# Low parts of weights in the mixers and the memory part: an accumulating DMA onto a negated high part in place of a subtraction

## The chip, the cores and the metric

The program runs on one core of a Trainium2 chip. A core has a matrix engine (TensorE, PE in the profile; its weight loads are the row PEld), a vector engine (VectorE, DVE), a scalar engine (ScalarE, ACT), a general engine (GpSimd, POOL) and a sync engine (SyncE, SP) that here issues the transfers. The metric is the time of one execution on the device in microseconds, less is better.

## The reference

Two encoder layers over x (512 tokens, 1024 features) with a memory of 256 tokens, then a final RMSNorm. All in float32.

```python
for i in range(DEPTH):                      # DEPTH = 2
    h = rms_norm(x, g_mix[i])
    if i % 2 == 0:                          # layer 0
        x = x + mixer_ab(h, w_in_ab[j], g_qa[j], g_ka[j], sink_b[j], w_out_ab[j], ang_1d, ang_2d)
    else:                                   # layer 1
        x = x + mixer_cd(h, w_in_cd[j], g_cq[j], g_ckv[j], w_uq[j], w_ukv[j], rpb_d[j], w_out_cd[j], ang_c)
    x = x + memory_cross_attention(rms_norm(x, g_xq[i]), rms_norm(mem, g_mem[i]),
                                   w_xq[i], w_xkv[i], w_xo[i])
    x = x + swiglu(rms_norm(x, g_ffn[i]), w_gate_up[i], w_down[i])
return rms_norm(x, g_final)
```

mixer_ab is two attentions side by side, A over all tokens with normed and rotated heads (8 heads, 2 of k and v) and B in a window of 128 tokens with a sink; both come from one input projection of 1536 columns and go through one output projection of 1024. mixer_cd is the same with C (latent attention, low-rank q and kv) and D (a 2-D neighbourhood with a bias). The cross-attention has 4 heads of 128 and projects the memory by w_kv (1024 x 1024) to keys and values. The FFN has 2816 columns for gate and as many for up.

## The kernel before

**Products of three.** Every float32 operand is split into a high part, which is the value rounded to the type float32r, and a low part, the rest. A product is three matmuls into one PSUM bank (`mm3`): high times high, high times low, low times high. On the profile's pages these are L127, L128 and L129.

**Weights.** `load` brings a piece of a weight matrix by one SP transfer into a tile `raw` (two buffers of 128 x 2048). `split` makes of 1024 columns of it the tiles `wh` and `wl`, each from a pool of four buffers: ACT copies raw to wh with the cast (L117), then DVE (one instruction) or POOL (four, one for each quarter) subtracts, wl = raw - wh (L123). So four splits can be in flight; a fifth waits until PE has read the buffer of the first for the last time. `alternate` takes turns between DVE and POOL where it is called: for the output projections ("op"), for the q and k weights of D ("dp") and for the memory's keys and values ("kv"). Everywhere else the low part is DVE's.

**Stages.** In each layer: norm of x and its split into xgh and xgl; input projection (by `natural_weights` and `natural` with tokens on the partitions, or, for D's q and k, by `proj_pair`); attention units that run score products, softmax (DVE, ACT, POOL), transposes of P on PE (L272) with a split of P into pth (ACT, L275) and ptl (DVE, L276), and PV products into the bank O (L550); `o_finish` (L236 ACT, L237 DVE) and the split of o into high (DVE, L293) and low (POOL, L294); output projection (`out_proj`), whose banks are added to x. The products on the memory (`memory_kv`, with casts of its results to kvh on ACT, L849) are run in the mixer, where PE has gaps. Then cross-attention and FFN, which have splits of their own for their weights. In layer 1 `v_d(0)` and `v_d(1)` are the values of D, their weights come from `natural_weights`.

**Order.** Each engine works through its instructions in a fixed order. It isn't that of the code: the framework simulates the program and sorts the instructions of all engines by the times that the simulation gives, so a change of one operation's kind can move others. PSUM has eight banks: two mm, two S, two T, one X and one O. SP issues only loads and stores and so runs ahead until a raw buffer is missing.

The line numbers here and in the rows are those of the kernel before; the changed kernel has them later in the file, by 11 behind `split` and by 15 behind `natural_weights`.

Of the kernel before, what the change touches and what calls it, by code (L numbers as in the profile page):

```python
# [11 lines left out]
F32R = mybir.dt.float32r  # L12
AF = mybir.ActivationFunctionType
ALU = mybir.AluOpType
# [3 lines left out]
P = 128  # L18
# [3 lines left out]
KF = D // P  # L22
# [9 lines left out]
def trunk_kernel(  # L32
# [6 lines left out]
    nc = tc.nc  # L39
# [4 lines left out]
    wp = ctx.enter_context(tc.tile_pool(name="wp", bufs=4))  # L44
    gp = ctx.enter_context(tc.tile_pool(name="gp", bufs=16))
    op = ctx.enter_context(tc.tile_pool(name="op", bufs=8))
# [51 lines left out]
    def load(src, a, b):  # L98
        raw = wp.tile([P, 2048], F32, tag="raw", bufs=2, name="raw")
        v = raw[:, :a * b].rearrange("p (a b) -> p a b", a=a)  # L100
        nc.sync.dma_start(v, src)
        return v
# [3 lines left out]
    def alternate(kind):  # L106

        turns[kind] = not turns.get(kind, False)
        return nc.vector if turns[kind] else nc.gpsimd

    def split(v, a, b, eng=None, low=nc.vector):
# [11 lines left out]
            low.tensor_sub(lv[:, q], v[:, q], hv[:, q].bitcast(F32))  # L123
        return hv, lv

    def mm3(o, lh, ll, rh, rl, start, stop):
        nc.tensor.matmul(o, lh, rh, start=start, stop=False)  # L127
        nc.tensor.matmul(o, lh, rl, start=False, stop=False)  # L128
        nc.tensor.matmul(o, ll, rh, start=False, stop=stop)  # L129
# [58 lines left out]
        return bc  # L188

    def natural_weights(w, c0, eng=None):  # L190
        v = load(w[:, c0:c0 + 256].rearrange("(k p) n -> p k n", p=P), KF, 256)
        return [split(v[:, 4 * i:4 * i + 4], 4, 256, eng) for i in range(2)]

    def natural(xh, xl, w, c0, evac, parts=None, bank_fn=None):

# [13 lines left out]
    def out_proj(os_, w, r0, after=None):  # L209

        nk = len(os_)
        for mg in range(2):
            v = load(w[r0:r0 + nk * P, mg * 512:(mg + 1) * 512]
                     .rearrange("(k p) n -> p k n", p=P), nk, 512)
            for mq in range(2):
                wh, wl = split(v[:, :, mq * 256:(mq + 1) * 256], nk, 256, None, alternate("op"))
                for m2 in range(2):
                    m = mg * 4 + mq * 2 + m2
                    bank = mm_bank()
                    cs = slice(m2 * P, (m2 + 1) * P)  # L220
                    for k in range(nk):
                        mm3(bank, wh[:, k, cs], wl[:, k, cs], *os_[k],
                            k == 0, k == nk - 1)
                    nc.vector.tensor_add(xs[m], xs[m], bank)
                    if after:
                        after(m)
# [78 lines left out]
    with tc.tile_pool(name="init", bufs=1) as ip:  # L305
# [17 lines left out]
        for f in range(KF):  # L323
            k = f % 2
            if f % 4 == 0:
                whl = [wp.tile([P, 1024], F32R, tag=t, name=t).rearrange("p (a b) -> p a b", a=4) for t in ("wh", "wl")]
            if k == 0:
                wh, wl = (t[:, f % 4:f % 4 + 2] for t in whl)
                v = raw[:, f:f + 2]
# [225 lines left out]
    def mixer_cd(normed, after):  # L555
# [3 lines left out]
        with tc.tile_pool(name="cd", bufs=2) as ph:  # L559
# [181 lines left out]
            def proj_pair(pr):  # L741

                if pr == 0:
                    qk = cT(4)
                else:
                    t = ph.tile([P, 4, S], F32R, tag="qk", bufs=2, name="dqk")
                    qk = [t[:, i] for i in range(4)]
                for w, c0, sc in ((0, 416, 0.125), (1, 928, 1.0)):
                    v = load(w_in[:, c0 + pr * P:c0 + (pr + 1) * P].rearrange("(k p) n -> p k n", p=P), KF, P)
                    wh, wl = split(v, KF, P, None, alternate("dp"))  # L750
                    bank = mm_bank()
                    for k in range(KF):
                        mm3(bank, wh[:, k], wl[:, k], xh[k], xl[k], k == 0, k == KF - 1)
                    t = (cT(1)[0].bitcast(F32) if pr == 0 else tmp())
                    nc.vector.scalar_tensor_tensor(t, bank, sc, bc, op0=ALU.mult, op1=ALU.mult)
                    nc.scalar.copy(qk[2 * w], t)
                    nc.gpsimd.tensor_sub(qk[2 * w + 1], t, qk[2 * w].bitcast(F32))
                return qk
# [58 lines left out]
    def memory_kv(layer):  # L817
# [34 lines left out]
            dst[1].append(l)  # L852

        for m2 in range(2):
            v = load(wkv[:, m2 * 256:(m2 + 1) * 256].rearrange("(k p) n -> p k n", p=P), KF, 256)
            bank = mm_bank()
            for m in range(2):
                wh, wl = split(v[:, :, m * P:(m + 1) * P], KF, P, None, alternate("kv"))
                for k in range(KF):
                    mm3(bank[:, m * MEM:(m + 1) * MEM], wh[:, k], wl[:, k], mh[k], ml[k],  # L860
                        k == 0, k == KF - 1)
            parts(bank.rearrange("p (m n) -> p m n", m=2), kT)

        for c in range(2):
            v = load(wkv[:, 512 + c * 256:512 + (c + 1) * 256].rearrange("(k p) n -> p k n", p=P), KF, 256)
            pr = [split(v[:, 4 * i:4 * i + 4], 4, 256, None, alternate("kv")) for i in range(2)]
            bank = mm_bank()
            for t in range(2):
                for k in range(KF):
                    wh, wl = pr[k // 4]  # L870
                    mm3(bank[:, t * 256:(t + 1) * 256], mh[k][:, t * P:(t + 1) * P],
                        ml[k][:, t * P:(t + 1) * P], wh[:, k % 4], wl[:, k % 4], k == 0, k == KF - 1)
            parts(bank.rearrange("p (t n) -> p t n", t=2), vm)
# [331 lines left out]
```

## Time and profile before

| | us |
|---|---|
| median of 3 runs | 1412.44 (1411.24 to 1412.59) |
| profiled execution | 1410.33 |
| its span, first to last instruction | 1408.3 |
| busy in the span: PE | 1374.1 (98%) |
| DVE | 796.6 (57%) |
| ACT | 632.8 (45%) |
| POOL | 413.1 (29%) |
| TensorE's clock granted, mean | 0.997 of full |

Layer 0's mixer takes the time to about 253 us, its cross-attention and FFN go to about 655; layer 1's mixer runs from there to about 969, the rest follows. The transfers move 120.88 MB in all, 86 GB/s in the mean. Busy times of one engine are sums over its instructions. A wait is the idle time of an engine right before an instruction, put to the one that released it.

### The profile page before, as it was taken

To read this page: it belongs to the slowest core of one execution; us is meant where nothing else is said; L and a number is where in the kernel's file an instruction comes from. 1 tells how busy PE (TensorE), PEld (TensorE's weight loads), DVE (VectorE), ACT (ScalarE), POOL (GpSimd) and SP (SyncE) were. 2 spreads that over 40 slices of the span, in tenths; PEclk is the share of its full clock that TensorE was granted. 3 is DMA by queue.
4 is the path that set the end of the run, shared out by engine and by line. 5 is a ranking of instruction groups with operands and counts; after the bars stand their busy time and mean duration, and the time that the engine had idled before them with its cause. 6 is when DMAs were issued, how large, how long until landed. Compare 5 with 4: busy or idle time off the path is not lost.

```text
span 1408.3 us, 20396 instructions
## 1 busy us (share of the span) xinstructions
PE 1374.1 (98%) x7835; PEld 1194.8 (85%) x7835; DVE 796.6 (57%) x1426; ACT 632.8 (45%) x1217; POOL 413.1 (29%) x503
## 2 busy tenths in 40 slices
PE   8898999999999999999999999999999999999997
PEld 8897889998888888888988888798988888888887
DVE  6988886763344334436578744657643353335355
ACT  5567785643221323323468554656533222222243
POOL 4855444212210121111324345752122111111121
PEclk9999999999999999999999999999999999999999
DMA  7110024321332223203221132324302322232111
GB/s 235 61 61 30 23 70 132 122 106 60 100 110 90 90 94 114 85 23 105 51 76 46 31 101 66 113 97 149 121 30 92 114 93 90 90 106 104 45 45 61
DMA packets 77514, 120.88 MB, mean 86 GB/s; under 512 B 5791, under 2 KB 64106, under 8 KB 71786
## 3 DMA queue, kind: packets, MB, share of 16 engines
q1 hardware_dynamic: 77418, 119.58, 26.3%
q8 instruction: 62, 1.02, 0.3%
q14 instruction: 34, 0.28, 0.1%
HBM read 117.47 MB, written 2.10 MB: 85 GB/s over the span
## 4 chain that ended last, share of the span: by engine, by line
PE 87%; DVE 8%; ACT 2%; issue 1%; DMA 1%; POOL 0%; SPq 0%; POOLq 0%; ACTq 0%; DVEq 0%
PE mm L127 12%; PE mm L128 12%; PE mm L129 12%; PE S L127 7%; PE S L128 7%; PE S L129 7%; PE T L128 6%; PE T L129 6%; PE T L127 6%; PE O L550 3%; PE T L272 2%; DVE wl L123 1%; PE X L129 1%; PE O L129 1%; PE X L127 1%
## 5 line engine op out<-in xcount | busy, mean ns | idle before, releaser
L117 ACT CAST wh<-rawgu 128x1024 fp32r<-128x1024 f32 x88 | 92.3, 1053 | 296.4 <-PE S L128 116.4
L117 ACT CAST wh<-raw 128x1024 fp32r<-128x1024 f32 (+2 forms) x116 | 115.0, 992 | 198.8 <-PE mm L128 53.4
L1029 POOL TENSOR_TENSOR act<-P,act 128x512 fp32r<-128x512 f32 x44 | 74.2, 1688 | 401.0 <-ACT act L1028 401.0
L127 PE MATMUL T<-xgh,wh 128*128 128x512 f32 x352 | 137.8, 391 | 0.0
L123 DVE TENSOR_TENSOR wl<-raw,wh 128x1024 fp32r<-128x1024 f32 (+2 forms) x98 | 123.3, 1260 | 24.8 <-ACT wh L117 23.5
L128 PE MATMUL S<-xgl,wh 128*128 128x512 f32 x352 | 137.2, 390 | 0.0
L127 PE MATMUL S<-xgh,wh 128*128 128x512 f32 x352 | 136.9, 390 | 0.1
L129 PE MATMUL S<-xgh,wl 128*128 128x512 f32 x352 | 137.0, 389 | 0.0
L129 PE MATMUL T<-xgh,wl 128*128 128x512 f32 x352 | 137.0, 389 | 0.0
L128 PE MATMUL T<-xgl,wh 128*128 128x512 f32 x352 | 136.9, 389 | 0.0
L123 DVE TENSOR_TENSOR wl<-rawgu,wh 128x1024 fp32r<-128x1024 f32 x88 | 116.4, 1325 | 28.5 <-ACT wh L117 27.9
L1025 DVE TENSOR_TENSOR P<-P,T 128x512 f32<-128x512 f32 x44 | 30.1, 688 | 138.5 <-PE T L129 137.1
L253 POOL TENSOR_SCALAR P<-P,sm 128x512 f32<-128x512 f32 (+2 forms) x128 | 81.5, 650 | 83.2 <-DVE sm L251 48.3
L1022 DVE TENSOR_TENSOR g<-S,bc 128x512 f32<-128x512 f32 x44 | 30.2, 691 | 130.5 <-PE S L129 124.9
L128 PE MATMUL mm<-act,wh 128*128 128x512 f32 (+1 forms) x264 | 99.0, 375 | 0.0
L127 PE MATMUL mm<-act,wh 128*128 128x512 f32 (+1 forms) x264 | 98.9, 375 | 0.0
L129 PE MATMUL mm<-act,wl 128*128 128x512 f32 (+1 forms) x264 | 98.8, 375 | 0.0
L276 DVE TENSOR_TENSOR ptl<-T,pth 128x512 fp32r<-128x512 f32 (+2 forms) x128 | 72.4, 583 | 21.1 <-ACT pth L275 20.7
L127 PEld LDWEIGHTS S<-xgh,wh 128*128 128x128 f32 x352 | 66.1, 188 | 14.7 <-DVE g L1022 0.9
L127 PEld LDWEIGHTS T<-xgh,wh 128*128 128x128 f32 x352 | 66.1, 188 | 14.2 <-issue 0.5
L128 PEld LDWEIGHTS T<-xgl,wh 128*128 128x128 f32 x352 | 66.1, 188 | 14.1 <-issue 0.5
L129 PEld LDWEIGHTS S<-xgh,wl 128*128 128x128 f32 x352 | 66.1, 188 | 13.7
(366 smaller groups left out, 3811.9 us busy)
## 6 DMA issues: line engine op xcount, KB each, us to landing
rawgu<-in_w_gate_up_dram SPq DMA_DIRECT2D x44, 1024.0 KB, 5.0
raw<-in_w_down_dram SPq DMA_DIRECT2D x16, 1024.0 KB, 5.2
raw<-in_w_xkv_dram SPq DMA_DIRECT2D x8, 1024.0 KB, 5.2
raw<-in_w_down_dram SPq DMA_DIRECT2D x8, 768.0 KB, 4.7
raw<-in_w_in_ab_dram SPq DMA_DIRECT2D x5, 1024.0 KB, 5.5
raw<-in_w_out_ab_dram SPq DMA_DIRECT2D x4, 1024.0 KB, 5.1
raw<-in_w_xq_dram SPq DMA_DIRECT2D x4, 1024.0 KB, 5.3
raw<-in_w_xo_dram SPq DMA_DIRECT2D x4, 1024.0 KB, 5.2
```

The costliest lines, as they stand in the source:

```text
L117: nc.scalar.copy(hv, v)
L123: low.tensor_sub(lv[:, q], v[:, q], hv[:, q].bitcast(F32))
L127: nc.tensor.matmul(o, lh, rh, start=start, stop=False)
L128: nc.tensor.matmul(o, lh, rl, start=False, stop=False)
L129: nc.tensor.matmul(o, ll, rh, start=False, stop=stop)
L253: nc.gpsimd.tensor_scalar(p, p, ri[:, j:j + 1], 1.0, op0=ALU.mult, op1=ALU.mult)
L272: nc.tensor.transpose(tb_[:, i * P:(i + 1) * P], p[:, i * P:(i + 1) * P], ident)
L276: nc.vector.tensor_sub(ptl[:, k0:k1, j * P:(j + 1) * P], tv, hv.bitcast(F32))
L550: nc.tensor.matmul(ob[:, q0 + a:q0 + b], v_of(kt), pt[:, kt, a:b], start=(i == 0 and j == 0), stop=(i == n - 1 and j == 1), skip_group_che ...
L1022: nc.vector.tensor_mul(g, bg, bc)
L1025: nc.vector.tensor_mul(sg, sg, bu)
L1029: nc.gpsimd.tensor_sub(l, sg, h.bitcast(F32))
```

## The change

A new function `split_by_dma` makes wh as before, by a copy with a cast on ACT. Then ACT writes the tile wl with the raw weights times -1, also rounded, so that it holds -wh; and a transfer that POOL issues adds the weights from DRAM to it, element by element: wl = -wh + w. It is called for 56 splits: all of `natural_weights` without a given engine (the second q part of A, kv of B and both q parts of B in layer 0; cq, ckv, v_d(0) and v_d(1) in layer 1; the memory's values in both layers), all of `out_proj` (16), `proj_pair` (8) and the memory's keys. 40 of the transfers have rows of 1 KB (128 x 4 x 256), 16 rows of 512 B (128 x 8 x 128). The splits of the cross-attention, of the FFN, of `up_pair`, the first kv weights of layer 0 and the q part with a given engine stay as they were.

```diff
+    def split_by_dma(v, a, b, src):
+
+        h = wp.tile([P, 1024], F32R, tag="wh", name="wh")
+        l = wp.tile([P, 1024], F32R, tag="wl", name="wl")
+        hv = h[:, :a * b].rearrange("p (a b) -> p a b", a=a)
+        lv = l[:, :a * b].rearrange("p (a b) -> p a b", a=a)
+        nc.scalar.copy(hv, v)
+        nc.scalar.activation(lv, v, AF.Copy, scale=-1.0)
+        nc.gpsimd.dma_start(lv, src, accum_op=ALU.add)
+        return hv, lv
...
     def natural_weights(w, c0, eng=None):
-        v = load(w[:, c0:c0 + 256].rearrange("(k p) n -> p k n", p=P), KF, 256)
-        return [split(v[:, 4 * i:4 * i + 4], 4, 256, eng) for i in range(2)]
+        src = w[:, c0:c0 + 256].rearrange("(k p) n -> p k n", p=P)
+        v = load(src, KF, 256)
+        if eng is not None:
+            return [split(v[:, 4 * i:4 * i + 4], 4, 256, eng) for i in range(2)]
+        return [split_by_dma(v[:, 4 * i:4 * i + 4], 4, 256, src[:, 4 * i:4 * i + 4]) for i in range(2)]
...
-                wh, wl = split(v[:, :, mq * 256:(mq + 1) * 256], nk, 256, None, alternate("op"))
+                cq = slice(mq * 256, (mq + 1) * 256)
+                wh, wl = split_by_dma(v[:, :, cq], nk, 256, src[:, :, cq])
...
-                    wh, wl = split(v, KF, P, None, alternate("dp"))
+                    wh, wl = split_by_dma(v, KF, P, src)
...
-                wh, wl = split(v[:, :, m * P:(m + 1) * P], KF, P, None, alternate("kv"))
+                wh, wl = split_by_dma(v[:, :, m * P:(m + 1) * P], KF, P, src[:, :, m * P:(m + 1) * P])
...
-            pr = [split(v[:, 4 * i:4 * i + 4], 4, 256, None, alternate("kv")) for i in range(2)]
+            pr = natural_weights(wkv, 512 + c * 256)
```

What stands in a row on the engines is shown for three places; names with a number are tiles.

ACT in layer 1, ahead of the values of D, where raw_7040 and its next hold the weights of v_d(0) (at 701 us in the profile). Before:

```order
L594 ACTIVATE P_6602<-mm_6784,sm_6580 128x256 x2
L595 ACTIVATE P_6834,sm_6833<-P_6602 128x256
L595 ACTIVATE P_6843,sm_6842<-P_6602 128x256
L117 CAST wh_7042<-raw_7040 128x1024
L594 ACTIVATE P_6603<-mm_6851,sm_6580 128x256 x2
L117 CAST wh_7046<-raw_7040 128x1024
L628 ACTIVATE cTh_6923<-X_6918,gcols_98 128x512
```

ACT at the same place in the changed kernel, where the weights are in raw_7044:

```order
L609 ACTIVATE P_6602<-mm_6788,sm_6580 128x256 x2
L610 ACTIVATE P_6838,sm_6837<-P_6602 128x256
L610 ACTIVATE P_6847,sm_6846<-P_6602 128x256
L133 ACTIVATE wl_7047<-raw_7044 128x1024
L132 CAST wh_7046<-raw_7044 128x1024
L133 ACTIVATE wl_7052<-raw_7044 128x1024
L609 ACTIVATE P_6603<-mm_6855,sm_6580 128x256 x2
L132 CAST wh_7051<-raw_7044 128x1024
L643 ACTIVATE cTh_6927<-X_6922,gcols_98 128x512
```

Both negations stand here, one ahead of the first cast and one ahead of the activation of P_6603 that followed the first cast.

ACT at the end of layer 0's mixer: pth are casts of the last unit's P, pair its output, kvh the memory's values (227 to 232 us). Before:

```order
L236 COPY pair_2728<-O_2702 64x512
L275 CAST pth_2731<-T_2733 128x3x128
L117 CAST wh_3232<-raw_3230 128x1024
L275 CAST pth_2731<-T_2739 128x2x128
L849 CAST kvh_3160<-mm_3111 128x512
L117 CAST wh_3277<-raw_3230 128x1024
L236 COPY pair_2728<-O_2744 64x512
L117 CAST wh_3328<-raw_3326 128x1024
L849 CAST kvh_3226<-mm_3177 128x512
L117 CAST wh_3374<-raw_3326 128x1024
```

ACT at the same place in the changed kernel:

```order
L251 COPY pair_2736<-O_2710 64x512
L290 CAST pth_2739<-T_2741 128x3x128
L133 ACTIVATE wl_3330<-raw_3327 128x1024
L132 CAST wh_3329<-raw_3327 128x1024
L290 CAST pth_2739<-T_2747 128x2x128
L133 ACTIVATE wl_3377<-raw_3327 128x1024
L865 CAST kvh_3228<-mm_3179 128x512
L132 CAST wh_3376<-raw_3327 128x1024
L251 COPY pair_2736<-O_2752 64x512
```

The copy of the last pair now stands behind the negation and the cast of the fourth quarter of the output projection's weights and behind kvh. On POOL five of the new transfers (wl_3175, wl_3235, wl_3281, wl_3330, wl_3377) stand in a row ahead of the low part of this last o, and on PE the unit's last six PV products stand behind the first nine products of the output projection instead of in the memory's products.

PE at the end of layer 1's mixer, in the memory's second keys product: m are its activations, O_9428 is the last attention unit's output (931 to 935 us). Before:

```order
L127 MATMUL mm_9791<-wh_9780,m_9619 128x256
L128 MATMUL mm_9791<-wl_9781,m_9619 128x256
L129 MATMUL mm_9791<-wh_9780,m_9619 128x256
L127 MATMUL mm_9791<-wh_9784,m_9625 128x256
L128 MATMUL mm_9791<-wl_9785,m_9625 128x256
L129 MATMUL mm_9791<-wh_9784,m_9625 128x256
```

PE at the same place in the changed kernel:

```order
L140 MATMUL mm_9790<-wh_9780,m_9621 128x256
L565 MATMUL O_9428<-pth_9415,vd_8504 128x256
L138 MATMUL mm_9790<-wh_9785,m_9627 128x256
L565 MATMUL O_9428<-ptl_9416,vd_8504 128x256
L565 MATMUL O_9428<-pth_9415,vd_8504 128x256
L565 MATMUL O_9428<-ptl_9416,vd_8504 128x256
L565 MATMUL O_9428<-pth_9415,vd_8504 128x128
L565 MATMUL O_9428<-ptl_9416,vd_8504 128x128
L139 MATMUL mm_9790<-wl_9786,m_9627 128x256
```

PV products stand ahead of the first product on the low part wl_9786 (L139), which was ahead of them before. On ACT there the negation into wl_9786 stands behind a cast of P, wh_9785 and kvh.

## Rows read from the trace of the kernel before

**Rows 1.** The page, busy us, share of the span and instructions of each engine.

```profile
PE 1374.1 (98%) x7835; PEld 1194.8 (85%) x7835; DVE 796.6 (57%) x1426; ACT 632.8 (45%) x1217; POOL 413.1 (29%) x503
```

**Rows 2.** Windows: stretch, its us, busy us of PE, PEld, DVE, ACT, POOL; clock; DMA.

```profile
20.00:110.00 90.00, 85.62 (x692) 82.42 (x690) 84.49 (x189) 50.96 (x109) 63.86 (x84) 1.00 0.25 80
110.00:145.00 35.00, 29.84 (x204) 25.94 (x203) 30.93 (x59) 28.35 (x66) 18.08 (x27) 0.95 0.10 31
126.00:130.00 4.00, 0.92 (x8) 0.81 (x8) 4.00 (x9) 1.35 (x4) 3.14 (x5) 0.99 0.43 125
130.00:133.00 3.00, 2.96 (x13) 2.69 (x14) 2.94 (x7) 2.30 (x7) 0.96 (x3) 0.50 0.54 183
210.00:240.00 30.00, 30.00 (x214) 28.09 (x214) 18.68 (x31) 16.79 (x29) 13.75 (x18) 1.00 0.45 141
```

**Rows 3.** Waits of PE: who, for whom, us in total, times, longest.

```profile
PE T L272 <- DVE ptl L276: 5.2, 4, 2.8
...
PE T L128 <- DVE wl L123: 0.3, 1, 0.3
```

**Rows 4.** Chain of waits in 20 to 130, its shares by line.

```profile
by line: DVE rt L366 6.9%; PE mm L127 6.7%; DVE rt L365 6.1%; PE mm L128 6.0%; DVE wl L123 6.0%; PE mm L129 5.9%; issue 5.7%; DVE sm L256 5.3%; DMA sink<-in_sink_b_dram 4.4%; DVE ptl L276 4.1%; DVE rt L367 3.2%; DVE nst L472 2.9%; PE S L492
```

**Rows 5.** Groups by form: count, busy us, mean ns of one, idle before.

```profile
L123 DVE TENSOR_TENSOR wl<-raw,wh 128x1024 fp32r<-128x1024 f32 x78 | 107.4, 1379 | 24.3 <-ACT wh L117 23.1
L117 ACT CAST wh<-raw 128x1024 fp32r<-128x1024 f32 x96 | 100.8, 1050 | 161.1 <-PE mm L128 47.3 <-PE T L128 30.8 <-PE S L128 30.7
L123 POOL TENSOR_TENSOR wl<-raw,wh 128x256 fp32r<-128x256 f32 x80 | 57.6, 751 | 34.1 <-ACT wh L117 34.1
L237 DVE TENSOR_TENSOR pair<-O,pair 64x512 f32<-64x512 f32 x32 | 21.8, 680 | 9.5 <-ACT pair L236 8.7
L236 ACT COPY pair<-O 64x512 f32<-64x512 f32 x32 | 18.7, 583 | 8.1 <-PE O L550 7.2
L294 POOL TENSOR_TENSOR o<-pair,o 128x512 fp32r<-128x512 f32 x13 | 16.9, 1296 | 33.7 <-DVE o L293 19.9 <-DVE sm L251 10.4 <-DVE sm L250 3.5
```

**Rows 6.** DMA issues: count, KB each, median us from issue to landing.

```profile
raw<-in_w_in_cd_dram SPq DMA_DIRECT2D x4, 1024.0 KB, 5.5
raw<-in_w_in_cd_dram SPq DMA_DIRECT2D x8, 512.0 KB, 3.9
...
P<-in_rope_a_dram SPq DMA_DIRECT2D x1, 256.0 KB, 7.5
```

**Rows 7.** SP's issues of one load: ns of one, least, median, most.

```profile
L101 SPq DMA_DIRECT2D raw<-in_w_in_cd_dram x12: 367/368/368, 655.0 to 822.2; - x12
```

**Rows 8.** Timeline at 701 to 704: start, us, engine, operation, idle before.

```profile
701.12 1.05 ACT L117 CAST wh<-raw 128x1024 fp32r<-128x1024 f32 x1 [2.69 <-PE mm L129]
...
702.20 1.23 DVE L123 TENSOR_TENSOR wl<-raw,wh 128x1024 fp32r<-128x1024 f32 x1 [2.46 <-ACT wh L117]
...
703.48 0.38 PE L128 MATMUL T<-wl,xgh 128*128 128x256 f32 x1 [0.28 <-DVE wl L123]
```

**Rows 9.** Timeline at 228 to 233, end of layer 0's mixer.

```profile
228.72 0.43 DVE L293 CAST o<-pair 128x512 fp32r<-128x512 f32 x1
...
229.74 0.28 PE L129 MATMUL mm<-wh,m 128*128 128x256 f32 x1
...
230.06 0.59 ACT L849 CAST kvh<-mm 128x512 fp32r<-128x512 f32 x1 [0.39 <-PE mm L129]
...
232.20 0.40 PE L128 MATMUL mm<-o,wh 128*128 128x512 f32 x1
```

**Rows 10.** Timeline at 929 to 935, end of layer 1's mixer.

```profile
929.17 0.37 ACT L275 CAST pth<-T 128x256 fp32r<-128x256 f32 x1
...
933.09 0.28 PE L128 MATMUL mm<-wl,m 128*128 128x256 f32 x1
...
933.90 0.28 PE L550 MATMUL O<-pth,vd 128*128 128x256 f32 x1
934.02 0.28 PE L550 MATMUL O<-ptl,vd 128*128 128x256 f32 x1
```

More of the change, by code (lines that the diff above doesn't have):

```diff
@@ L212, in out_proj @@
         for mg in range(2):
-            v = load(w[r0:r0 + nk * P, mg * 512:(mg + 1) * 512]
-                     .rearrange("(k p) n -> p k n", p=P), nk, 512)
+            src = w[r0:r0 + nk * P, mg * 512:(mg + 1) * 512].rearrange("(k p) n -> p k n", p=P)
+            v = load(src, nk, 512)
             for mq in range(2):
-                wh, wl = split(v[:, :, mq * 256:(mq + 1) * 256], nk, 256, None, alternate("op"))
+                cq = slice(mq * 256, (mq + 1) * 256)
+                wh, wl = split_by_dma(v[:, :, cq], nk, 256, src[:, :, cq])
                 for m2 in range(2):
@@ L748, in proj_pair @@
                 for w, c0, sc in ((0, 416, 0.125), (1, 928, 1.0)):
-                    v = load(w_in[:, c0 + pr * P:c0 + (pr + 1) * P].rearrange("(k p) n -> p k n", p=P), KF, P)
-                    wh, wl = split(v, KF, P, None, alternate("dp"))
+                    src = w_in[:, c0 + pr * P:c0 + (pr + 1) * P].rearrange("(k p) n -> p k n", p=P)
+                    v = load(src, KF, P)
+                    wh, wl = split_by_dma(v, KF, P, src)
                     bank = mm_bank()
@@ L854, in memory_kv @@
         for m2 in range(2):
-            v = load(wkv[:, m2 * 256:(m2 + 1) * 256].rearrange("(k p) n -> p k n", p=P), KF, 256)
+            src = wkv[:, m2 * 256:(m2 + 1) * 256].rearrange("(k p) n -> p k n", p=P)
+            v = load(src, KF, 256)
             bank = mm_bank()
             for m in range(2):
-                wh, wl = split(v[:, :, m * P:(m + 1) * P], KF, P, None, alternate("kv"))
+                wh, wl = split_by_dma(v[:, :, m * P:(m + 1) * P], KF, P, src[:, :, m * P:(m + 1) * P])
                 for k in range(KF):
@@ L864, in memory_kv @@
         for c in range(2):
-            v = load(wkv[:, 512 + c * 256:512 + (c + 1) * 256].rearrange("(k p) n -> p k n", p=P), KF, 256)
-            pr = [split(v[:, 4 * i:4 * i + 4], 4, 256, None, alternate("kv")) for i in range(2)]
+            pr = natural_weights(wkv, 512 + c * 256)
             bank = mm_bank()
```

## The prediction

> **What bounds the kernel now.** I read the page's busy times first: PE is busy 1374.1 us of the span of 1408.3 [rows 1], so all other engines together can give back at most 34 us, and a low part that comes late costs only if PE runs out of work. Next the stretches [rows 2]. In the mixer of layer 0 PE is idle for 4.4 us of 20 to 110 and for 5.2 of 110 to 145, and there DVE is the partner that is full: 84.5 us of 90, and in 126 to 130 4.00 of 4.00 while PE does 0.92. Behind that gap TensorE's clock is granted at 0.50 (the lower of its two levels, 1.2 GHz) from 130 to 133, some 3.4 us in all, which costs another 1.7. Third, PE's own waits: low parts of P on DVE (L276) 5.2 us, and low parts of weights (L123), the thing that is changed, 0.3 us in one place [rows 3]. So the subtractions are not waited for. They matter as DVE's load: of the chain that leads through 20 to 130 the DVE subtractions of weights are 6.0%, 6.6 us [rows 4].
>
> **The change, part by part.** *Instructions.* 56 splits lose their subtraction: 36 on DVE, 20 on POOL (80 pieces). By [rows 5] that is 36 x 1.38 = 50 us less on DVE and 80 x 0.75 = 60 less on POOL, of which PE saw 0.3. Added are 56 negating passes on ACT, each taken as a cast of the same shape, 1.05 us: 59 us on an engine that is 45% busy [rows 1], and 56 transfers of 512 KB issued by POOL. Raw weights are still loaded, so 28 MB are read a second time.
>
> *Two unknown prices.* No row of before shows POOL issuing a transfer, or one that adds. Price c, POOL's time for an issue: the nearest row is SP's, 0.37 us [rows 7], the other end is the work that it replaces, four pieces of 0.75 = 3.0 us [rows 5]; between them I take the middle, 1.7. Price L, from issue to landing: a plain 512 KB load takes 3.9 us, 1024 KB 5.5, so 512 KB more of data cost 1.6 [rows 6]. An adding transfer must fetch the destination as well, so I take 3.9 + 1.6 = 5.5; bounds are 3.9 (the add is free) and 7.5 (the longest load shown). It is nearest to the 1024 KB row, which moves as much.
>
> The Trainium skill has for this path, in "DMA: Bandwidth & Descriptors", section "Anatomy of one DMA — SWDGE (gpsimd) path", 2.0 us plus bytes over 436 GB/s; an estimate from that is 3.2 us for 512 KB, by which the two terms that hang on L below would be 1.9 and 0. No row here shows such a transfer. The same skill, in "Collectives: The Full Stack", section "The bandwidth ceiling: the fold count and why AG ≠ RS ≠ AR", says that an add needs two source reads and so runs at half the rate, which speaks for the doubled data term.
>
> *Most splits are covered.* A subtraction took 1.2 to 3 us; negation plus transfer take 1.05 + c-issue + 5.5. Four splits may be in flight, and between the end of a low part and PE's first product on it I read mostly 6 to 65 us (each DVE or POOL instruction of L123 set beside PE's first product on the same tile, 56 pairs; the rows leave the buffer numbers out, so the three short ones stand below in their place). At L = 5.5 that hides some 53 of the 56; if the cover is gone each would cost what exceeds it, up to 5.5 - 1.2 = 4 us. Three places are not covered.
>
> *T1, layer 1 at 703* [rows 8]. The two halves of v_d(0)'s weights are split while PE has little else: the cast starts at 701.12, the subtraction ends at 703.4, and PE's first product on it starts at 703.48, 0.28 late already. Now ACT's negation can start at 701.1 when the buffer comes free, ends at 702.2, and the sum lands at 702.2 + 5.5 = 707.7: **+4.2** (2.6 at 3.9, 6.2 at 7.5). The second half's transfer is in flight beside the first and lands during PE's next 18 products (2.2 us).
>
> *T2, end of layer 0's mixer, at 232* [rows 9]. ACT's negations now stand in a row ahead of casts for the last attention unit, and the last PV products move behind nine of the output projection. PE's last product of the memory part is at 229.74; ten of the projection's start by 232.20, so one is 0.235. On ACT: negation 229.9 to 230.95 (it waits for the buffer that PE has just left), kvh 0.59 to 231.5, wh 1.05 to 232.6. PE's PV end at 229.86 + 9 x 0.235 + 6 x 0.12 = 232.7; the copy of the pair takes 0.58 behind that, DVE's sum 0.68, its cast 0.43, POOL's low part 1.30 [rows 5, 9]: 235.7 with the passing on. PE has nine other products until 234.8 and two more on the high part until 235.25, so about **+0.7** with the passing on, whatever L is, as long as POOL's five issues ahead of that low part are out by 234.5.
>
> *T3, end of layer 1's mixer, at 933* [rows 10]. ACT's cast of P ends at 929.54; behind it stand wh 1.05, kvh 0.58 and the negation 1.05: 932.2, and the sum lands at 937.7. PE wanted that low part at 933.09; 17 PV products (one each 0.12: 933.90 to 934.02) and 8 transposes that are now ahead put this off by 2.4 us, to 935.4. So **+2.3** (0.7 at 3.9, 4.3 at 7.5).
>
> *T4, relief in layer 0's mixer.* Ten DVE subtractions, 13 us, leave 20 to 121, where DVE is 94% busy. On the chain they are 6.6 us [rows 4]. If all of PE's idle time there went, and the half clock with it, 4.4 + 5.2 + 1.7 = 11.3 would come back, of which I drop 0.4 as the start's own; nothing at all if the RoPE, norm and softmax rows of DVE simply close up behind other waits, and a loss if POOL is the next bound (below). ACT gets a second pass in each of these splits and POOL an issue in the same chain, so I take half of the 6.6: **-3.3**.
>
> Sum: 4.2 + 0.7 + 2.3 - 3.3 = +3.9 on the profiled execution's 1410.33 (span 1408.3), 1414.2. It lies 2.1 below the median 1412.44, so on the median's scale 1412.4 + 3.9 = **1416**. The FFNs keep their splits and stay as they are.
>
> **The rivals.** *R1, the relief wins.* If c is near SP's 0.37 and L near 3.9, DVE's load falls by 13 of 84 and T4 gives its whole 10.9, while T1 to T3 cost 2.6 + 0.7 + 0.7: -6.9, **1405**. For it: DVE is the full engine, 4.00 of 4.00 right ahead of the half-clock stretch [rows 2], and the chain shows it. Against it: only 6.6 us of the chain are these subtractions, the others are RoPE and softmax rows that stay.
>
> *R2, POOL becomes the bound* (slower). POOL is busy 63.9 us of 90 in 20 to 110 [rows 2], with RoPE and headnorm work that PE waits for through DVE; it loses one split there (3 us) and gets ten issues. It is full from c = (90 - 61) / 10 = 2.9 us on. With c = 5 the load is 61 + 50 = 111 of 90: +21, the relief is gone, and the 7.2 of T1 to T3 stay: +28, **1441**. The same happens if the transfers, not the issues, pile up: from 210 to 240 the queues are busy at 0.45 [rows 2], and eight adding transfers more would about double that. For it: each transfer is 512 or 1024 pieces of 1 KB or 512 B, and POOL has shown no such work. Against it: SP issues the same pattern in 0.37.
>
> The Trainium skill has a rule that speaks for R2, in "SBUF — State Buffer", in the box on DVE blocking DMA: a transfer issued by GpSimd gets its descriptors written by that engine, and stands still while DVE holds the port that they share in a 2-port operation. With DVE 94% busy from 20 to 110 it would stretch each of the ten issues; no run here shows it yet.
>
> *R3, a balance.* T4 gives 7 instead of 3.3 and the three places cost the same 7.2: within 0.2%, **1412**. Also the case if transfers are covered everywhere and DVE's gaps stay: PE is at 98% and nothing shows.
>
> **How the numbers follow.** A measurement of this kernel can tell about 0.2% from no change, 2.8 us: 1409.6 to 1415.3. My forecast, +3.9 with L or c as taken or worse but POOL not full (1415.3 to 1430), has 0.38; R2 0.18; R3 0.18; R1 0.26. Faster is R1, 0.26; same is R3, 0.18; slower is the forecast and R2, 0.56. The forecast's own range is 1413 (L = 3.9: 2.6 + 0.7 + 0.7 - 3.3 = +0.7) to 1424 (L = 7.5 without relief: 6.2 + 0.7 + 4.3 = +11.2). For 8 in 10 it must take in half of R1 and half of R2: 1403 to 1440.
>
> **What would show it.** In the profile after: PE's products at the T1 place waiting some 4 us for a transfer into wl, and at T3 some 2; at T2 a wait for the low part of o on POOL under 1 us. The issue's time on POOL and the landing of 512 KB are read straight from the list of transfers. For T4: DVE's busy time in 20 to 110 falls to about 73, PE's idle time in 20 to 145 from 9.6 us to about 6. R1 is right if PE's idle time there is under 2 and the granted clock stays at 1.00 in 126 to 133; R2 if POOL is busy nearly all of 20 to 110 and PE waits for RoPE rows or for wl in layer 0. The forecast is wrong if landing takes under 3 us or over 8, if one issue costs POOL over 2.9 us, or if any transfer beside the three places is waited for over 1 us.

## The result and the profile after

The changed kernel takes 1434.72 us (median of 4 runs) where the kernel before took 1411.84 in the same measurement: a ratio of 1.0164, 95% interval 1.0147 to 1.0182, +22.9 us. The prediction's direction and its wide range held (1403 to 1440); its sum was +3.9, and most of this section's rows are about the other 19. The profiled execution's span is 1432.9 us, 24.6 more than before.

The page's first part, beside [rows 1], and its part on queues (packets, MB, share of 16 engines' span; q1 is SP's, q0 POOL's):

```profile
PE 1384.6 (97%) x7835; PEld 1203.2 (84%) x7835; DVE 758.5 (53%) x1390; ACT 681.5 (48%) x1273; POOL 425.3 (30%) x479
...
q1 hardware_dynamic: 77418, 119.58, 25.8%
q0 software_dynamic: 37760, 29.36, 14.4%
```

DVE lost 38 us of busy time and ACT gained 49 (counted: 50 and 59). POOL has not been relieved: its 80 pieces are gone, and with the 56 issues it is busy 12 us longer than before. PE does the same 7835 products but is busy 10.5 us longer, which is the first sign of a slower clock; its idle time grew by 14.1 us. The transfers on q0 hold the queues for 14.4% of 1432.9 us = 206 us, 3.7 us for each of the 56; SP's loads need 25.8% for 119.58 MB, 1.6 us for as many bytes.

Windows of the changed kernel, columns as in [rows 2]; the last three are stretches at half clock:

```profile
20.00:110.00 90.00, 83.43 (x631) 79.92 (x631) 73.50 (x172) 55.69 (x110) 64.12 (x86) 0.92 0.61 132
110.00:145.00 35.00, 30.79 (x215) 27.27 (x214) 28.02 (x58) 28.46 (x65) 20.34 (x26) 0.95 0.32 70
210.00:240.00 30.00, 27.10 (x223) 26.61 (x222) 11.95 (x29) 22.77 (x44) 13.48 (x14) 1.00 0.94 191
700.00:730.00 30.00, 25.05 (x186) 24.40 (x185) 7.51 (x28) 14.62 (x40) 7.83 (x14) 0.89 0.42 88
...
136.00:139.20 3.20, 3.20 (x10) 2.52 (x9) 1.91 (x4) 1.34 (x3) 1.90 (x3) 0.50 0.81 276
716.40:722.80 6.40, 5.04 (x23) 5.04 (x24) 0.83 (x3) 1.44 (x2) 1.63 (x4) 0.50 0.84 145
924.60:931.00 6.40, 6.40 (x29) 5.63 (x27) 3.99 (x13) 3.71 (x10) 4.59 (x7) 0.50 0.69 105
```

DVE did fall to 73.5 us of 90 in 20 to 110, just as forecast (73), and yet PE is idle for 6.6 us there (4.4 before), and for 10.8 in 20 to 145 (9.6 before, about 6 forecast). The queues' share went from 0.25 to 0.61, and in 210 to 240 from 0.45 to 0.94. The clock: before had one half-clock stretch in the body of the run, 3.4 us; after has five, of 6.8, 6.8, 3.4, 6.8 and 6.8 us (from 36.9, 71.0, 135.9, 716.2 and 924.4), so 27.3 us more at half clock, worth up to 13.6. Only the one from 716.2 begins in a wait for a low part. In 20 to 145 no low part is waited for at all; the longest of PE's waits there are for the three other engines:

```profile
PE S L507 <- ACT P L260: 2.2, 2, 1.3
PE mm L138 <- DVE o L308: 1.8, 1, 1.8
PE T L287 <- POOL P L268: 1.6, 1, 1.6
```

Ahead of the stretch from 924.4 they are two of 0.7 us, for POOL and DVE.

Waits of PE in the whole run, beside [rows 3] (us in total, times, longest):

```profile
PE mm L139 <- DMA wl<-in_w_xkv_dram: 6.6, 4, 2.0
PE T L139 <- DMA wl<-in_w_in_cd_dram: 4.9, 1, 4.9
```

Transfers into wl now stand at the head of the list, with 11.5 us, where the subtractions had 0.3. The four waits of the first line, from the timeline:

```profile
225.53 0.39 PE L139 MATMUL mm<-wl,m 128*128 128x256 f32 x1 [1.58 <-DMA wl<-in_w_xkv_dram]
...
234.19 0.38 PE L139 MATMUL mm<-wl,m 128*128 128x256 f32 x1 [1.32 <-DMA wl<-in_w_xkv_dram]
...
957.84 0.39 PE L139 MATMUL mm<-wl,m 128*128 128x256 f32 x1 [1.68 <-DMA wl<-in_w_xkv_dram]
...
965.86 0.39 PE L139 MATMUL mm<-wl,m 128*128 128x256 f32 x1 [2.00 <-DMA wl<-in_w_xkv_dram]
```

Behind none of these four does a half-clock stretch begin.

Where the 24.5 us arose can be read by setting the start of PE's n-th product in one trace against the n-th in the other. (The order differs in places, so inside a mixer the n-th product need not be the same one, and such a reading can be off by some 2 us; at the end of a mixer the same products lie behind.) The changed kernel is 6 us behind by 93 us, wins 3 back by 123, and is 10.6 behind at the end of layer 0's mixer. It gains 1.2 in the first products of layer 1, loses 7.2 at v_d(0), 4.6 from there to 921 and 3.3 to the mixer's end: 24.5, which then stays to the end. So the FFNs are untouched; layer 0 cost 10.6 and layer 1 13.9.

The two prices that no row of before showed, from the line of the new transfers (ns least/median/most on POOL; us from issue to landing least/median/most), and the landing by tensor:

```profile
L134 POOL DMA_DIRECT2D wl<-in_w_xkv_dram x16: 1273/1434/1595, 167.6 to 956.7; - x16
L134 POOL DMA_DIRECT2D wl<-in_w_in_ab_dram x8: 1312/1330/1811, 24.7 to 71.6; - x8
...
DMA to landing us min/median/max: 5.8/7.7/14.2
```

```profile
wl<-in_w_xkv_dram POOLq DMA_DIRECT2D x16, 512.0 KB, 7.6
wl<-in_w_in_cd_dram POOLq DMA_DIRECT2D x16, 512.0 KB, 7.6
wl<-in_w_in_ab_dram POOLq DMA_DIRECT2D x8, 512.0 KB, 8.6
wl<-in_w_out_ab_dram POOLq DMA_DIRECT2D x8, 512.0 KB, 6.4
```

An issue costs POOL 1.3 to 1.8 us, 1.32 in the median of all 56 (taken: 1.7). Landing takes 7.7 in the median, at the upper bound and not the 5.5 taken, and up to 14.2.

Two more things changed that the sum did not have. First, loads by SP that share the queues with the new transfers land later: those of w_xq, which come next behind the output projections, took 5.3 us in the median before and take 10.1 now. Second, DVE's products of RoPE, 0.2 to 0.8 us each before, take up to 3.7 us now. The four longest (1.7 to 3.7 us) each begin while POOL issues a transfer. Before and after, and the longest of them with its issue:

```profile
L366 DVE TENSOR_TENSOR rt<-rt,tb_s x12: 209/454/825, 63.6 to 125.7; 128x128 f32<-128x128 f32 x8, 128x64 f32<-128x64 f32 x4
...
L381 DVE TENSOR_TENSOR rt<-rt,tb_s x12: 209/483/3686, 63.1 to 134.2; 128x128 f32<-128x128 f32 x8, 128x64 f32<-128x64 f32 x4
...
103.13 1.28 POOL L134 DMA_DIRECT2D wl<-in_w_out_ab_dram  x1 [2.75 <-ACT wl L133]
...
103.57 3.69 DVE L381 TENSOR_TENSOR rt<-rt,tb_s 128x128 f32<-128x128 f32 x1
```

DVE's busy time shows it too: in the run below that has the negation but no transfer, its 1390 instructions take 746.6 us, the 50 less that were counted, and none of these products takes over 0.84; here as many instructions take 758.5. What PE lost by it no run tells apart.

### The profile page after: what moved, and what is told of

Read it like the earlier page. It is cut to its first block, busy times and chain, and to the rows that moved or that the text cites. A ratio compares the mean times of both kernels' runs of the same rounds, so it can differ in the third digit from the quotient of the medians.

```text
span 1432.9 us, 20410 instructions
## 1 busy us (share of the span) xinstructions
PE 1384.6 (97%) x7835; PEld 1203.2 (84%) x7835; DVE 758.5 (53%) x1390; ACT 681.5 (48%) x1273; POOL 425.3 (30%) x479
## 3 DMA queue, kind: packets, MB, share of 16 engines
q1 hardware_dynamic: 77418, 119.58, 25.8%
q0 software_dynamic: 37760, 29.36, 14.4%
## 4 chain that ended last, share of the span: by engine, by line
PE 84%; DVE 5%; ACT 4%; DMA 3%; issue 2%; POOL 1%; SPq 0%; ACTq 0%; POOLq 0%; DVEq 0%
PE mm L138 12%; PE mm L139 11%; PE mm L140 11%; PE S L138 7%; PE S L139 7%; PE S L140 7%; PE T L139 6%; PE T L140 6%; PE T L138 6%; PE O L565 2%; PE T L287 2%; DMA wl<-in_w_xkv_dram 1%; DMA raw<-in_w_in_ab_dram 1%; ACT P L260 1%; ACT wl L133 1%
## 5 line engine op out<-in xcount | busy, mean ns | idle before, releaser
L139 PE MATMUL S<-xgl,wh 128*128 128x512 f32 x352 | 137.2, 390 | 0.0
L139 PE MATMUL T<-xgl,wh 128*128 128x512 f32 x352 | 137.0, 389 | 0.0
L117 ACT CAST wh<-raw 128x1024 fp32r<-128x1024 f32 (+3 forms) x60 | 56.2, 940 | 165.1 <-PE S L139 46.1
L139 PE MATMUL mm<-act,wh 128*128 128x512 f32 (+1 forms) x264 | 99.0, 375 | 0.0
L123 DVE TENSOR_TENSOR wl<-raw,wh 128x1024 fp32r<-128x1024 f32 (+3 forms) x62 | 77.2, 1248 | 7.5 <-ACT wh L117 4.6
L139 PEld LDWEIGHTS T<-xgl,wh 128*128 128x128 f32 x352 | 66.1, 188 | 14.1 <-issue 0.5
L138 PEld LDWEIGHTS T<-xgh,wh 128*128 128x128 f32 x352 | 66.1, 188 | 14.1 <-issue 0.5
```

The source lines that it names most:

```text
L117: nc.scalar.copy(hv, v)
```

## The experiments

Theory A at the start: the new cost is that PE waits for low parts which land late, and that such idle time brings half-clock stretches, on top of a relief of DVE that is real. Rivals: ACT's second pass (C), POOL's issue (D), the queues' load (F). I took the new split apart in steps.

**A ladder.** Of `split_by_dma` first nothing, then the negation, then a transfer that overwrites:

```diff
 # lad0_no_low                        # lad1_neg_only: the transfer's line left out
-        nc.scalar.activation(lv, v, AF.Copy, scale=-1.0)
-        nc.gpsimd.dma_start(lv, src, accum_op=ALU.add)
-        return hv, lv
+        return hv, hv
 # lad2_plain
-        nc.gpsimd.dma_start(lv, src, accum_op=ALU.add)
+        nc.gpsimd.dma_start(lv, src)
```

> The changed kernel with no low part made at all in the 56 splits: no subtraction, no negation, no transfer; the products use the high part a second time, so the output is not the reference's. It is the floor of any way of making the low part. Theory A (DVE is the partner that holds PE up in layer 0's mixer, and the new cost is all in what replaces the subtraction): PE's idle time in 20 to 145 falls from 9.6 to under 5 us, half-clock stretches go, about 1402 to 1406 us. Rival B (relieving DVE is worth nothing, other waits close up): 1410 to 1413.

> The changed kernel without the 56 transfers: ACT still writes the negated high part, which then stands in for the low part, so the output is not the reference's. Theory A (transfers cost, ACT's pass doesn't): within 2 us of the run without low parts. Rival C (ACT's second pass, 56 x 1.05 us in front of softmax casts, is what costs): more than 8 us above the run without low parts.

> The changed kernel with a transfer that overwrites in place of one that adds: same bytes from DRAM, same issue on POOL, same negation ahead of it; the low part then holds the raw weights, so the output is not the reference's. Theory A (lateness and queue share of an adding transfer, 7.7 us to landing where 3.9 to 5.5 were expected): landing falls to about 5 us, queue time to less than half, time about 1420 (two of the four new half-clock stretches stay, with the wait at v_d(0)). Rival D (POOL's issue of 1.3 to 1.6 us, the same in both, is the price): within 3 us of 1434.

Measured: 1393.48 us (0.9875 of before, 0.986 to 0.989), 1404.71 (0.9951, 0.9935 to 0.9968), 1422.44 (1.0079, 1.0061 to 1.0097), and the changed kernel 1434.72. Dropping the subtractions alone is worth 18 us, more than the theory said and against rival B. Then each step takes some: the negation 11.2, the plain transfer 17.7, the add 12.3. Theory A's "within 2 us" for the negation fell and rival C's "more than 8 us" held; rival D's "within 3 us" of the changed kernel fell, the add is a price of its own. For the plain transfer theory A came near (1422 for 1420, landing 5.5 for 5), but the queue time fell to 72% and not "to less than half", and all four new half-clock stretches stay, though shorter (17 us in all). No single step is the whole cost. The last step is the cleanest: lad2 and the changed kernel have, by lines and tile names, the same order of instructions on PE, DVE, ACT and POOL throughout. At the other steps the framework also sorted the engines anew (of 7835 products of PE 5906 keep their place in the row from lad0 to lad1, 5950 from lad1 to lad2), so 11.2 and 17.7 hold the price of a new order too, which no run takes out. Windows of lad0, lad1 and lad2 in this order, 20 to 110 and 110 to 145 each:

```profile
20.00:110.00 90.00, 89.03 (x724) 86.03 (x723) 79.84 (x194) 56.74 (x126) 60.43 (x86) 1.00 0.25 80
110.00:145.00 35.00, 34.59 (x257) 31.51 (x255) 32.27 (x73) 32.11 (x78) 18.40 (x26) 1.00 0.10 31
```

```profile
20.00:110.00 90.00, 87.72 (x719) 85.80 (x718) 74.96 (x184) 63.53 (x131) 56.97 (x82) 1.00 0.26 82
110.00:145.00 35.00, 32.77 (x227) 27.73 (x226) 30.06 (x64) 31.38 (x70) 18.05 (x25) 1.00 0.10 31
```

```profile
20.00:110.00 90.00, 83.48 (x639) 80.08 (x639) 71.15 (x172) 56.69 (x112) 60.06 (x86) 0.94 0.49 133
110.00:145.00 35.00, 30.40 (x225) 27.18 (x224) 29.22 (x60) 29.06 (x65) 19.36 (x26) 1.00 0.23 68
```

Without low parts PE's idle time in 20 to 145 is 1.4 us and the clock stays at 1.00: DVE's subtractions did hold PE up there. With ACT's negation it is 4.5, with the transfer 11.1. By 138 us PE is ahead of before by 12.0, 6.8 and behind by 3.0; at the end of layer 0's mixer, ahead by 12.2, 3.9 and behind by 5.8, where the changed kernel is 10.6 behind. By 93 us lad2 is as late as the changed kernel (6.1 and 5.8) and lad1 1.8 ahead of before: the start of layer 0 pays for the transfer as such (or for the order that came with it), the add is paid for at the mixers' ends and at v_d(0). The price of the add, from the line of the transfers in lad2:

```profile
L134 POOL DMA_DIRECT2D wl<-in_w_xkv_dram x16: 740/874/972, 166.4 to 948.0; - x16
...
DMA to landing us min/median/max: 3.9/5.5/12.0
```

So POOL's issue of a plain transfer of these weights is 0.74 to 0.97 us, of an adding one 1.27 to 1.60, and landing of all 56 is 5.5 against 7.7. Their share of the queues is 10.4% of 1421.4 us, 2.6 us for each of 56, against 3.7.

**The wait at v_d(0) undone.** `natural_weights` gets a flag, and v_d(0)'s two splits are DVE's again:

```diff
-                natural(xh, xl, w_in, 1440 + grp * 256, v_evac, None, bank_fn)
+                natural(xh, xl, w_in, 1440 + grp * 256, v_evac,
+                        natural_weights(w_in, 1440 + grp * 256, sub=not grp), bank_fn)
```

> The changed kernel with the two splits of v_d(0)'s weights made by DVE's subtraction again. Theory A (the wait there costs its idle 4.9 us and, behind it, some 2.6 us of a half-clock stretch that the idle time brings): 7.2 us less, 1427.5, and the half-clock stretch near 716 is gone. Rival E (the half clock there does not come from the wait): 4.9 us less, 1430, the stretch stays.

1426.17 us, 8.5 less than the changed kernel. In its window PE is idle for 0.3 us and the clock is whole, where the changed kernel had 0.89 and 5 us of idle time:

```profile
700.00:730.00 30.00, 29.72 (x250) 29.51 (x249) 14.30 (x40) 16.31 (x46) 5.72 (x14) 1.00 0.21 63
```

Theory A holds here: with the wait the half clock goes too. A wait of 4.9 us cost 7.2. The other runs agree: wherever PE waits for this low part (4.9 us in the changed kernel, 3.2 in lad2, 4.8 and 2.6 in two runs below, natural_weights alone and the negation on DVE) a half-clock stretch begins between 711 and 716 us; in the runs below that keep the subtraction there, none does.

**Each place alone.** Four kernels change one caller each, the others keep `split`.

> Only the 16 splits of the mixers' natural_weights are changed (8 at the start of layer 0, 8 in layer 1); output projections, D's q and k and the memory part keep their subtractions. Theory A (each place pays its own price, the prices add up): the start of layer 0 5 us with its two half-clock stretches, the wait at v_d(0) 7, so 1423 to 1425. Rival F (the price is the load of 56 transfers together on the queues): under 1418, since 16 of 56 transfers are left.

> Only the 16 splits of the output projections are changed. Theory A: 1 to 3 us more than before, 1413 to 1415, from ACT's passes in front of the last unit of each mixer. Rival G (where leads are long the relief of DVE and POOL wins): 1407 or less.

> Only the 16 splits of the memory part are changed (8 in each layer, of which four waits of PE, 6.6 us in all, come in the changed kernel). Theory A: 4 to 7 us more than before, 1416 to 1419. Rival F (the waits come from the output projection's transfers that share the queues with them): under 1413.

> Only the 8 splits of D's q and k weights are changed (layer 1, rows of 512 B). Theory A: no wait of PE for one of them shows in the changed kernel, so within 2 us of before, 1410 to 1414. Rival G (relief): 1408 or less.

| changed alone | splits | us | ratio to before, interval | over 1410.75 |
|---|---|---|---|---|
| natural_weights in the mixers | 16 | 1422.53 | 1.0084 (1.0069 to 1.0099) | +11.8 |
| output projections | 16 | 1416.81 | 1.0045 (1.003 to 1.006) | +6.1 |
| memory part | 16 | 1419.84 | 1.0064 (1.0049 to 1.0079) | +9.1 |
| D's q and k | 8 | 1413.37 | 1.0019 (1.0009 to 1.0028) | +2.6 |

Together 29.6 against 22.9 for all at once, so each place has a price of its own and all loads together are no worse than their parts: rival F, as put, falls in the first and third. That the prices add up, as theory A has it, holds only to within these 6.7 us. No place gains, against rival G. Two sizes were off: the output projections cost 6.1, not 1 to 3, and the memory part 9.1, not 4 to 7. In the first, PE waits for something I had not looked for, DVE's add of a bank to x, ahead of the second projection's products in each layer:

```profile
242.56 0.47 PE L138 MATMUL mm<-o,wh 128*128 128x512 f32 x1 [1.98 <-DVE x L237]
...
962.02 0.47 PE L138 MATMUL mm<-dT,wh 128*128 128x512 f32 x1 [2.12 <-DVE x L237]
```

What made these adds late stands in the traces of ACT and DVE, and in the landing of the load of w_xq before and in this run:

```profile
238.25 1.05 ACT L117 CAST wh<-raw 128x1024 fp32r<-128x1024 f32 x1 [4.06 <-DMA raw<-in_w_xq_dram]
...
239.33 1.23 DVE L123 TENSOR_TENSOR wl<-raw,wh 128x1024 fp32r<-128x1024 f32 x1 [3.51 <-ACT wh L117]
...
241.74 0.68 DVE L237 TENSOR_TENSOR x<-x,mm 128x512 f32<-128x512 f32 x1
```

```profile
raw<-in_w_xq_dram SPq DMA_DIRECT2D x4, 1024.0 KB, 5.3
...
raw<-in_w_xq_dram SPq DMA_DIRECT2D x4, 1024.0 KB, 12.2
```

The loads of the next stage's weights, in flight beside the last adding transfers, land after 12.2 us instead of 5.3; ACT's cast waits for it, DVE's subtraction for the cast, and the add stands behind the subtraction in DVE's order. Behind PE's wait a half-clock stretch of 3.4 us begins at 244.0. At 957 to 962 the same chain stands again (4.36 us of ACT, 3.77 of DVE). So the queues' load does cost time, here with eight transfers in each layer. In the three runs without transfers at this place (lad1, the memory part alone, D's q and k alone) these loads land after 5.1 to 5.4 us.

And in the memory part alone PE waits for a low part once, 0.9 us; its longest new wait is 1.8 us for the low part of layer 0's last o, on POOL. POOL had been idle for 6.3 us ahead of that, waiting for DVE's high part, which waited for ACT's copy of the pair, which waited 3.5 us for PE: the order of PE itself, which now has this unit's last PV products behind the projection's first ones, makes this wait. No transfer of another part is there to cause it. Behind this wait, too, a half-clock stretch of 3.4 us begins, at 238.8.

**Lateness against load.** All negations and adding transfers stay, but PE reads the high part in place of the low one:

```diff
         nc.gpsimd.dma_start(lv, src, accum_op=ALU.add)
-        return hv, lv
+        return hv, hv
```

> The changed kernel with all its negations and adding transfers, but PE reads the high part a second time in place of the low part, so nothing waits for a transfer except the buffer's next use; the output is not the reference's. It parts lateness from load. Theory A (PE waits for low parts that land late, and the half clock follows): at most 1412, no more than 7 us above the run with the negation alone (1404.7). Rival F (load: POOL's issues and the share of the queues, which hold up rope rows and raw weights): 1425 or more.

1449.37 us (1.0271, 1.0257 to 1.0285), 14.7 slower than the changed kernel. That is inside rival F's "1425 or more", but slower than the kernel that was to be explained, which neither theory allows for. The run doesn't part the two, and shows why in ACT's waits:

```profile
ACT wl L133 <- DMA raw<-in_w_in_cd_dram: 11.6, 6, 4.0
...
ACT wl L133 <- DMA raw<-in_w_xkv_dram: 10.1, 5, 4.0
...
ACT wl L133 <- DMA wl<-in_w_in_cd_dram: 6.9, 3, 4.4
...
ACT wl L133 <- DMA wl<-in_w_in_ab_dram: 5.2, 1, 5.2
```

A low part that nobody reads gives its buffer back early, and in the framework's new order ACT stands in front of its negations until the raw weights have come (46.9 us over five tensors, of which two are shown) or the transfer into the same buffer has landed (12.1). The casts and exponents of the softmax queue behind. PE's longest wait becomes 4.3 us for P from ACT. What it does show: late loads and transfers also cost through another engine that waits in order, not only through PE. How much of the start of layer 0 is the queues' load and how much POOL's issues stays open. Of the two, the trace of the changed kernel shows little of the first there (in 20 to 145 ACT waits for a raw weight once, 0.6 us) and the longer RoPE products of the second.

**The negation on another engine.**

```diff
-        nc.scalar.activation(lv, v, AF.Copy, scale=-1.0)
+        nc.vector.tensor_scalar_mul(lv, v, -1.0)
```

> The changed kernel with the 56 negations on DVE in place of ACT; transfers and casts as they are. The run with negations alone was 11.2 us slower than the one without low parts. Theory J (that price is ACT's: its negation and cast stand in a row in front of rope's casts and the softmax): 5 to 9 us less than the changed kernel, 1426 to 1430, and the half-clock stretch near 37 is gone. Rival K (the price is that of a pass on any engine and of two steps in series): 1432 to 1437. Rival L (DVE, full in layer 0, gives back its relief, and its passes hold up the descriptors that POOL writes): 1440 or more, with POOL's issue well above 1.3 us.

1424.71 us (1.0094, 1.0077 to 1.011), 10.0 less than the changed kernel. Its rows, the negation (ns least/median/most) and the transfer's issue:

```profile
L133 DVE TENSOR_SCALAR wl<-raw x56: 672/694/1829, 22.4 to 960.9; 128x1024 fp32r<-128x1024 f32 x56
...
L134 POOL DMA_DIRECT2D wl<-in_w_xkv_dram x16: 1273/1569/1767, 170.4 to 946.1; - x16
```

Against rivals K and L, theory J's direction holds, a little beyond its range: most of what the negation costs is a price of ACT. How much of that is its place in front of other casts, how much its 1.06 us where DVE needs 0.69, and how much the new order of all engines, this run doesn't part. Not all as expected: a half-clock stretch near 38 stays, at 3.4 us, and in the first 93 us this kernel is 7 us behind even the changed one; it has won that back by 138, and wins from there at the ends of both mixers. An issue became a little longer while DVE negates, 1.57 against 1.43 in the median.

**A version with only the places that gain.** PE's lag showed gains at 93 to 130 and at 650 to 683, so the subtractions of before come back everywhere except in layer 0's first output projection (mix_op0) and, in a second kernel, cq's and ckv's weights (mix_op0_c):

```diff
-            out_proj(sa["out"], w_out, 0)
+            out_proj(sa["out"], w_out, 0, by_dma=True)
...
-            natural(xh, xl, w_in, 256, ckv_evac)
+            natural(xh, xl, w_in, 256, ckv_evac, natural_weights(w_in, 256, by_dma=True))
```

> The kernel before with only the four splits of layer 0's first output projection (around 90 to 130 us, where DVE is full and the run that changed the output projections alone gained 2.5 us by 133) made by a transfer. Theory A (long lead, DVE relieved): 1407.5 to 1409.5, 1.5 to 3 us less than before. Rival H (start-up differences of the runs, not the change, made that gain): within 1 us of before.

> As mix_op0, and the four splits of cq's and ckv's weights at the start of layer 1, where the changed kernel lost 1.2 to 1.4 us of its lag against before. Theory A: another 1.3 us less, 1406 to 1408. Rival I (the transfers there make the raw weights of v_d(0) or its low part late): 2 us or more above mix_op0.

1411.09 (0.9996, 0.9987 to 1.0005) and 1409.69 (0.999, 0.9981 to 0.9999). The first is no change (rival H), the second about 1.9 us less, at the edge of what can be told and short of the 3.6 to 5.6 expected. The gain that I had read at 93 to 130 was in part the comparison by n-th products: by the end of layer 0's mixer mix_op0 is 0.2 us behind. So of the versions tried none clearly beats the kernel before, and the one that comes nearest keeps eight splits of 56.

## Why the prediction was right, and where it was not

**The direction and T1 to T3: right, by the mechanism named; the range: in part luck.** The measured time lies above the forecast's own range (1413 to 1424) and above the 1430 up to which its chance was put. It is inside 1403 to 1440 because the range took in half of R2, whose first mechanism did not come. And one of the prediction's own signs of being wrong, a wait of over 1 us beside the three places, came three times. T1, v_d(0), as it went:

```profile
710.35 1.06 ACT L133 ACTIVATE wl<-raw 128x1024 fp32r<-128x1024 f32 x1 [2.57 <-PE mm L139]
...
711.72 1.34 POOL L134 DMA_DIRECT2D wl<-in_w_in_cd_dram  x1 [3.03 <-ACT wl L133]
...
717.76 0.58 PE L139 MATMUL T<-wl,xgh 128*128 128x256 f32 x1 [4.86 <-DMA wl<-in_w_in_cd_dram]
```

The negation waits for the buffer, the sum lands 6 us behind the issue, PE waits 4.86 (forecast 4.2). The product then takes 0.58 and not 0.38 as in [rows 8]: the clock fell to half at 716.2, after PE had stood still from 712.9, and that made 7.2 of 4.9. This second half was not in the sum, though the prediction read just such a stretch in [rows 2] and counted what its going would give back. T2's wait for the low part of o on POOL is 0.62 (0.7), and comes from the PV products that moved back on PE, as said; ACT, which the forecast had down as busy until then, stood idle for 0.35 us when they ended. T3 is the wait at 957.84, 1.68 (2.3). The three places with the half clock at T1 make some 9.5 us; the other 15 were not in the sum. (The product at T3 is the memory's first values product; the words ahead of the prediction call it one of keys.)

**Price c: right** (1.3 to 1.8, taken 1.7). POOL stayed at 64 us of 90 in 20 to 110, so R2 by its first mechanism, a full POOL, did not happen. Its second one, transfers that pile up, did: the share in 210 to 240 "would about double" from 0.45, and is 0.94. The time came near R2's 1441, but that the piling up is what brought it there is shown only for the output projections alone, by the late loads of w_xq. With the 56 negations on DVE an issue went from 1.43 to 1.57 us in the median and landing from 7.7 to 7.5, so of the rule in the box on DVE blocking DMA (the Trainium skill, "SBUF — State Buffer", section "SBUF: two separate sides") the trace shows a tenth of an issue at most.

**Price L: mis-sized,** 5.5 taken, 7.7 measured. The data part (3.2 for twice the bytes; the queues' time for one is 3.7) was near. The rest, 2.3 from SP's row, was not: POOL's issue alone takes a microsecond more than SP's 0.37, and the transfers met others in the queues. The estimate from the Trainium skill's "DMA: Bandwidth & Descriptors", section "Anatomy of one DMA — SWDGE (gpsimd) path", 3.2 us for 512 KB, is under every landing here: 3.9 at least and 5.5 in the median for the plain transfers of lad2. The half rate of an add, which the Trainium skill's "Collectives: The Full Stack", section "The bandwidth ceiling: the fold count and why AG ≠ RS ≠ AR", states for the adding step of a collective, is a larger loss than these runs show: queue time 3.7 against 2.6 us, a factor of 1.4. At 7.7 the covered splits are fewer. The step that failed with it is "Most splits are covered": beside T3 the second low part of each other values product of the memory is waited for, 1.58, 1.32 and 2.00 us at 225.5, 234.2 and 965.9, and the forecast counted all three as covered. There the buffers turn in a ring: a split can't start before PE has left the one four earlier. ACT's cast, which in the changed order stands ahead of the negation, waits for that in layer 1 for 0.9 us each time, and for 0.5 in the first of layer 0; from the start of the negation, issue and landing then take 10.5 to 10.9 us at these four places, in place of the subtraction's 1.2 to 3.

**T4: the relief, failed.** Taken -3.3, and R1 had -10.9. The relief is there: 12.0 us by 138 us in the run without low parts. In the changed kernel the negation and the transfers ate it and 4 us more by 138. That ACT's pass would enter the same chain was said, and half of 6.6 us was taken off for it and for POOL's issue; the run with the negation alone shows 5.2 of these 12 gone by 138 and 8.2 by the end of layer 0's mixer. Beyond that half the 59 us of ACT work had no price, on the strength of ACT's 45% [rows 1], and ACT's share over the whole span says nothing on an engine with RoPE casts and softmax in order behind the negation. In the chain of 20 to 130 of the changed kernel, beside [rows 4], DVE's subtraction (6.0%) is gone from the front and the negation stands there with 3.6%. (The 5.4% of raw weights are one load that began at 14.96 us, ahead of the first new transfer at 24.65.)

```profile
by line: PE mm L138 11.2%; PE mm L139 10.4%; PE mm L140 10.0%; DVE rt L381 7.4%; DVE sm L271 5.9%; DMA raw<-in_w_in_ab_dram 5.4%; DMA sink<-in_sink_b_dram 5.1%; issue 3.7%; DVE rt L380 3.7%; ACT wl L133 3.6%; PE O L565 3.5%; DVE ptl L291 3.
```

## What to carry to other kernels

An engine that is 45% busy over the run can still be the one that a stage waits for: price a second pass by the in-order queue that it joins, with what stands behind it. A step that replaces a 1 to 3 us operation by one with 8 us of latency needs buffers for the difference, and a ring of four that PE drains just in time has none. Ask of a new transfer not only when it lands but which loads share the queues with it: here those of the next stage took 12.2 us instead of 5.3. And price a new wait of the matrix engine with the half-clock stretch that may follow: here 4.9 us of waiting cost 7.2, while behind waits of 1.3 to 2.0 us such a stretch began in two runs (the output projections alone, the memory part alone) and in the changed kernel did not.

## What the runs showed of the hardware

POOL's issue of an adding transfer of 512 KB takes 1.27 to 1.81 us and of a plain one 0.74 to 0.98, against SP's 0.37 [rows 7]. The adding one lands after 7.7 us in the median (5.8 to 14.2), the plain one after 5.5 (3.9 to 12.0). SP's 1024 KB loads of w_xq landed after 10.1 (changed kernel) and 12.2 us (output projections alone) in the median beside them, after 5.3 before. Negating 128 x 1024 floats takes DVE 0.69 us and ACT 1.06. A product of RoPE on DVE, 0.83 us at most before, took up to 3.69 where it began during an issue on POOL. TensorE's half-clock stretches in the body of the runs lasted 3.4 or 6.8 us and, in the runs of natural_weights alone and of unread low parts, 10.2 us.
